# Weight-sum jobs summed one step behind their loads, with the full-size loads on GpSimd's queue

## The chip, the cores and the metric

The kernel runs on one core of a Trainium2 chip. The metric is the device time of one execution in microseconds; three runs of the kernel before took 1957.03, 1960.13 and 1961.34 us.

## The reference

One layer of a decoder for 1024 prompt tokens and 8 x 4 sample tokens, in float32. What matters here are its matrix products:

```python
h = rmsnorm(x, norm1_g) * (1.0 + sc1) + sh1
u = h @ w_in                      # u_x, u_g, u_q, u_k, u_v, u_r, u_lr, u_ga, u_gb
...                               # y_a: recurrent branch (conv, two gates per block, scan)
...                               # y_b: gated linear attention branch
m = sigmoid(u_ga) * (y_a @ proj_a) + sigmoid(u_gb) * (y_b @ proj_b)
x = x + gt1 * (m @ w_out)
h2 = rmsnorm(x, norm2_g) * (1.0 + sc2) + sh2
f1, f2 = split(h2 @ ffn_w1, 2)    # 22 tiles of 128 columns each
x = x + gt2 * ((silu(f1) * f2) @ ffn_w2)
```

## The kernel before

**Two halves.** The tokens are done in two halves: `A` (512 prompt tokens) and `B` (512 prompt tokens and the 32 sample tokens). Each half runs `begin` or the norm, `branches` (projections, attention, recurrent branch, `merge_b`, `merge_a`) and `back` (w_out, second norm, FFN). In the trace, tile names of half A end in a, those of half B in b.

**Three matmuls for one.** A float32 product is made of three matmuls: each weight tile is loaded into a buffer "raw" (512 KB as a rule), and split there into a high part (ScalarE, L154) and a low part (VectorE, L155), written to one of three "hl" buffers. `gemm` (L452 to L454) multiplies high by high, high by low and low by high. The raw buffer is free when the split is done, the hl buffer when the matmuls that read it are.

**Weight sums.** The products marked fast (`ffn1_fast`, `ffn2_fast`, `gates_fast`) multiply 2 x 2 blocks with seven products in place of eight. They need sums and differences of weight blocks. These are made once, while other stages run, and kept in DRAM (`wsum`, `wsumg`, `wsum2`). A *job* loads two weight tiles r1 and r2, does four additions on VectorE and stores both back:

- *Full-size jobs*, `weight_sums` (L348): for FFN tiles f = 6 to 21, two loads of 512 KB through SyncE's queue (`load_raw`, L145; the trace calls the tiles s_raw), sums in L352 to L355, two stores through GpSimd's queue (L356, L357). One `next(sums_of)` does all of it. They use the same five raw buffers as the weight loads.
- *Half-size jobs*, `paced_sums` (L362): twenty jobs for FFN tiles 4 and 5, the gate weights and part of the FFN's second weights, in two buffers of their own (tag "sums"). Loads go through GpSimd's queue (L388) behind a one-column copy (L387) from the tile that `pace` names, so that they do not start before that tile exists. One `next(sums_late)` does the loads, the next one the sums (L392 to L396) and stores (L398).

**Where the jobs are done.** `merge_b` (L1182) goes through j = 0 to 7: a gate product (gbps, the tile for j + 1 in half A), then the product with proj_b (pbps) and the join (L1211). In half A the remaining steps of the recurrent branch run between these: products ux and ug, and for every pair of blocks two small gate loads of 128 KB (lwa_raw, also in raw buffers; the matmuls of L1094 read the raw buffer itself). `merge_a` (L1273, half A) goes through j = 0 to 7: a gate product (gaps), two products with halves of proj_a (papsa with pa0 and pa1), the join and `keep_m`. Full-size jobs are done in half A alone: in `merge_b` at j = 0 to 6, in `merge_a` at j = 0, 1, 3, 4 and 6, and in the first FFN output product (`ffn2(0, 11)`, called in `back`, L1644) at j = 0, 2, 4 and 6. Half-size jobs are loaded and summed in `merge_b` (half A: j = 3 to 6; half B: every j) and `merge_a` (half A: j = 1 to 4) or `merge_a_fast` (half B).

**What sets the order.** Each engine has one list of instructions that it runs in order, and the framework writes the lists: at each point it takes, of the instructions that can run by its own estimates, the one that stands first in the program. A tile's buffer is given out when it is first written and is free after its last use. `behind(n)` holds an instruction on its engine behind the last one that the program wrote before it: in the half-size jobs it keeps the first addition from moving ahead. The first addition of a full-size job had no such hold. `as_written` fixes the order of the matmuls in the fast products, not in the two merges of half A.

Of the kernel before, what the change touches and what calls it, by code (L numbers as in the profile page):

```python
# [7 lines left out]
F32 = mybir.dt.float32  # L8
# [7 lines left out]
P = 128  # L16
# [38 lines left out]
def hybrid_layer(ctx, tc, I, O):  # L55
# [292 lines left out]
    def weight_sums():  # L348

        for f in range(FAST[0], NF):  # L350
            r1, r2 = load_raw(I["ffn1"][2 * f], 1024, f"s1{f}"), load_raw(I["ffn1"][2 * f + 1], 1024, f"s2{f}")
            dve.tensor_add(r2[:, 512:1024], r2[:, 0:512], r2[:, 512:1024])  # L352
            dve.tensor_sub(r2[:, 0:512], r1[:, 0:512], r2[:, 0:512])
            dve.tensor_sub(r1[:, 0:512], r2[:, 512:1024], r1[:, 0:512])
            dve.tensor_sub(r1[:, 512:1024], r1[:, 512:1024], r1[:, 0:512])  # L355
            pool.dma_start(wsum[f][:, 0:1024], r1)  # L356
            pool.dma_start(wsum[f][:, 1024:2048], r2)  # L357
            yield 1
# [3 lines left out]
    def paced_sums():  # L362
# [20 lines left out]
        for k, (u, src, to) in enumerate(jobs):  # L383
            r = [wp.tile([P, 768], F32, tag="sums", name=f"sums{k}{v}", bufs=2) for v in range(2)]
            rv = [t[:, :2 * u].rearrange("p (n u) -> p n u", n=2) for t in r]
            for v in range(2):
                pool.tensor_copy(r[v][:, 0:1], pace[0][:, 0:1])  # L387
                pool.dma_start(rv[v], src[v])  # L388
            yield 1
            r1, r2 = rv  # L390
            last = len(traced())
            dve.tensor_add(r2[:, 1], r2[:, 0], r2[:, 1])  # L392
            behind(last)
            dve.tensor_sub(r2[:, 0], r1[:, 0], r2[:, 0])
            dve.tensor_sub(r1[:, 0], r2[:, 1], r1[:, 0])
            dve.tensor_sub(r1[:, 1], r1[:, 1], r1[:, 0])  # L396
            for v in range(2):
                pool.dma_start(to[v], rv[v])  # L398
            yield 1

    sums_of, sums_late = weight_sums(), paced_sums()

    class Half:
# [778 lines left out]
        def merge_b(s):  # L1182
# [14 lines left out]
            for j in range(KD):  # L1197
# [3 lines left out]
                if s.hf or 3 <= j < 7:  # L1201
                    pace[0] = tgs[j]
                    next(sums_late, None)
# [9 lines left out]
                if s.hf or 3 <= j < 7:  # L1213
                    next(sums_late, None)
                if s.hf == 0 and j < 7:
                    next(sums_of, None)
# [56 lines left out]
        def merge_a(s):  # L1273
            s.m = []
            for j in range(KD):
                tg = s.gate_a(j)
                if 1 <= j < 5:
                    next(sums_late, None)
                s.join(j, tg, s.over(tg, s.branch_a(j)))
                s.keep_m(j)  # L1280
                if 1 <= j < 5:
                    next(sums_late, None)
                if j % 3 < 2 and j < 7:
                    next(sums_of, None)
# [537 lines left out]
```

## Time and profile before

| | |
|---|---|
| median of three runs | 1960.13 us (1957.03 to 1961.34) |
| profiled execution | 1958.39 us, its span 1956.6 us |
| mean granted TensorE clock | 0.997 |
| busy, share of the span | PE 98%, PEld 90%, DVE 70%, ACT 50%, POOL 7% |
| moved by DMA | 319 MB, mean 163 GB/s |
| `merge_b` of half A | about 259 to 453 us of the span |
| `merge_a` of half A | 452 to 559 us |
| `ffn2(0, 11)` of half A | 728 to 789 us |

A page of the profile and its views name a group of instructions by line, engine, operation and tiles, "out<-in". PE is the matmul queue of TensorE, PEld its weight loads, DVE VectorE, ACT ScalarE, POOL GpSimd, SP SyncE; a q behind the name means the engine's sequencer or its DMA queue. A list of waits has: who waited, for whom, microseconds in total, times, the longest. In a timeline, the square bracket is the idle time before an instruction and what ended it.

### The profile page before, as it was taken

The numbers are of one execution on the slowest core, as the hardware profiler recorded it, in microseconds if no ns is written. First come the engines' busy times: TensorE is split into PE (matmuls) and PEld (weight loads), VectorE is DVE, ScalarE is ACT, GpSimd is POOL, SyncE is SP. The second block draws the span as 40 slices with busy tenths as digits, with TensorE's granted clock in tenths as the row PEclk, the third lists the DMA queues.
The fourth block names the chain that finished last, engine by engine and source line by source line (L and its number), as shares of the span: only waits on it lengthen the run. The fifth ranks groups of instructions, "written<-read, shape, count | busy, mean of one in ns | idle before, by whom it ended". The sixth has DMA issues, their size and how long they took to land. (4 is left out here: it accounts for less than half of the span.)

```text
span 1956.6 us, 33960 instructions
## 1 busy us (share of the span) xinstructions
PE 1923.5 (98%) x13380; PEld 1754.8 (90%) x13380; DVE 1360.1 (70%) x2420; ACT 972.6 (50%) x1559; POOL 144.6 (7%) x279
## 2 busy tenths in 40 slices
PE   8999999998999999999999999999999999999997
PEld 5877777787899998998899998999999999999997
DVE  5648587765658774677664497786467688888867
ACT  4536376552235552555353366675245354656653
POOL 0000002111200000000000101031201000000000
PEclk9999999999999999999999999999999999999999
DMA  8344326567864467554331413334447534555553
GB/s 342 116 154 172 117 90 245 176 211 240 292 201 157 129 184 243 193 183 149 119 123 65 146 50 101 124 114 153 140 143 226 198 130 133 176 171 179 177 163 104
DMA packets 122240, 319.24 MB, mean 163 GB/s; under 512 B 14560, under 2 KB 29664, under 8 KB 122080
## 3 DMA queue, kind: packets, MB, share of 16 engines
q1 hardware_dynamic: 107536, 263.89, 41.6%
q0 software_dynamic: 14000, 52.62, 7.5%
q8 instruction: 105, 1.72, 0.4%
q10 hardware_dynamic: 544, 0.56, 0.1%
q14 instruction: 55, 0.45, 0.1%
HBM read 278.42 MB, written 38.59 MB: 162 GB/s over the span
## 5 line engine op out<-in xcount | busy, mean ns | idle before, releaser
L155 DVE TENSOR_TENSOR fwa_hl<-fwa,fwa_hl 128x1024 fp32r<-128x1024 f32 (+1 forms) x57 | 68.8, 1207 | 44.6 <-ACT fwa_hl L154 41.2
L155 DVE TENSOR_TENSOR fwb_hl<-fwb,fwb_hl 128x1024 fp32r<-128x1024 f32 (+1 forms) x64 | 77.2, 1207 | 27.7 <-ACT fwb_hl L154 27.4
L154 ACT ACTIVATE fwa_hl<-fwa 128x1024 fp32r<-128x1024 f32 (+1 forms) x57 | 59.3, 1040 | 44.0 <-PE fapsa L1436 10.8
L154 ACT ACTIVATE fwb_hl<-fwb 128x1024 fp32r<-128x1024 f32 (+1 forms) x64 | 66.6, 1041 | 23.4 <-PE fcpsb L1436 9.0
L452 PE MATMUL f3psa<-faa,f3a_hl 128*128 128x512 f32 x176 | 68.6, 390 | 0.6 <-ACT f3a_hl L154 0.6
L454 PE MATMUL f3psa<-faa,f3a_hl 128*128 128x512 f32 x176 | 68.5, 390 | 0.4 <-DVE f3a_hl L155 0.4
L453 PE MATMUL f3psa<-faa,f3a_hl 128*128 128x512 f32 x176 | 68.6, 390 | 0.0
L154 ACT ACTIVATE f3a_hl<-f3a_raw 128x768 fp32r<-128x768 f32 (+1 forms) x32 | 25.3, 792 | 55.7 <-PE f3psa L454 47.3
L155 DVE TENSOR_TENSOR f3a_hl<-f3a_raw,f3a_hl 128x768 fp32r<-128x768 f32 (+1 forms) x32 | 28.3, 888 | 17.0 <-ACT f3a_hl L154 16.7
L452 PEld LDWEIGHTS f3psa<-faa,f3a_hl 128*128 128x128 f32 x176 | 33.0, 188 | 7.8 <-ACT f3a_hl L154 1.0
L454 PEld LDWEIGHTS f3psa<-faa,f3a_hl 128*128 128x128 f32 x176 | 33.0, 188 | 7.6 <-DVE f3a_hl L155 0.9
L453 PEld LDWEIGHTS f3psa<-faa,f3a_hl 128*128 128x128 f32 x176 | 33.0, 188 | 6.8
L352 DVE TENSOR_TENSOR s_raw<-s_raw 128x512 f32<-128x512 f32 x16 | 11.1, 691 | 40.2 <-DMA s_raw<-in_ffn 40.2
L454 PE MATMUL wopsb<-mb,wob_hl 128*128 128x272 f32 x128 | 36.9, 288 | 0.0
L452 PE MATMUL wopsb<-mb,wob_hl 128*128 128x272 f32 x128 | 36.9, 289 | 0.0
L453 PE MATMUL wopsb<-mb,wob_hl 128*128 128x272 f32 x128 | 36.8, 288 | 0.0
L453 PE MATMUL wopsa<-ma,woa_hl 128*128 128x256 f32 x128 | 36.4, 284 | 0.0
L454 PE MATMUL wopsa<-ma,woa_hl 128*128 128x256 f32 x128 | 36.2, 283 | 0.0
L452 PE MATMUL wopsa<-ma,woa_hl 128*128 128x256 f32 x128 | 36.1, 283 | 0.0
L1621 POOL DMA_DIRECT2D out_yb<-yb x4 | 2.9, 720 | 407.5 <-DVE yb L1618 406.8
L452 PE MATMUL uxpsa<-h1a,uxpsa_hl 128*128 128x512 f32 x80 | 32.3, 403 | 0.0
L155 DVE TENSOR_TENSOR fvb_hl<-fvb,fvb_hl 128x768 fp32r<-128x768 f32 x28 | 26.8, 956 | 7.7 <-ACT fvb_hl L154 7.4
(2404 smaller groups left out, 7975.3 us busy)
## 6 DMA issues: line engine op xcount, KB each, us to landing
ada<-in_ada_w SPq DMA_DIRECT2D x48, 512.0 KB, 5.5
fwb<-wsum SPq DMA_DIRECT2D x72, 256.0 KB, 3.6
s_raw<-in_ffn SPq DMA_DIRECT2D x32, 512.0 KB, 4.1
wsum<-s_raw POOLq DMA_DIRECT2D x32, 512.0 KB, 3.9
fwa<-wsum SPq DMA_DIRECT2D x64, 256.0 KB, 3.3
fwb<-in_ffn SPq DMA_DIRECT2D x54, 256.0 KB, 3.6
fwa<-in_ffn SPq DMA_DIRECT2D x48, 256.0 KB, 3.2
woa_raw<-in_w_out SPq DMA_DIRECT2D x13, 512.0 KB, 3.5
```

Source lines behind the costliest of these rows:

```text
L154: act.activation(hl[:, 0, :n], raw[:, :n], AF.Copy)
L155: dve.tensor_sub(hl[:, 1, :n], raw[:, :n], hl[:, 0, :n].bitcast(F32))
L352: dve.tensor_add(r2[:, 512:1024], r2[:, 0:512], r2[:, 512:1024])
L452: pe.matmul(out, wh, x[:, o:o + w], start=st, stop=False)
L453: pe.matmul(out, wh, x[:, N + o:N + o + w], start=False, stop=False)
L454: pe.matmul(out, wl, x[:, o:o + w], start=False, stop=en)
L1621: (queues[j // 2 % len(queues)]).dma_start(out[:, j:j + 2, o:o + w], y2)
```

## The change

A class `Jobs` steps through a list of jobs: `step` does the sums and stores of the job begun in the step before, and then begins the next one (its loads); `finish` does the last sums. Full-size and half-size jobs both go through it, so each job is summed one step behind its loads.

- A full-size job loads r1 and r2 through GpSimd's queue in place of SyncE's, into the same five raw buffers, without a pacing copy. Its first addition is now held by `behind`.
- A half-size job keeps its two buffers, queue and pacing copy.
- `merge_b`, half A: full-size steps at j = 0 to 6 and a `finish` at j = 7; half-size steps at j = 3 to 7 (five begin, four are summed). Half B: one half-size step at each j, ahead of the product with proj_b.
- `merge_a`: half-size steps at j = 0, 1, 2 and a `finish` at j = 3; full-size steps at j = 0 to 4 and a `finish` at j = 5.
- `merge_a_fast`: one step after each of the four gate groups, and a `finish` after the loop; before, jobs also went on at j >= 4.
- `ffn2(0, 11)`: steps at j = 0, 2, 4, 6 and a `finish` behind the loop.

```diff
--- before.py
+++ after.py
@@ -345,17 +345,39 @@
 
         return t[:, :HP].rearrange("p (m u n) -> p m u n", u=2, n=P)[:, :, u, :]
 
-    def weight_sums():
-
-        for f in range(FAST[0], NF):
-            r1, r2 = load_raw(I["ffn1"][2 * f], 1024, f"s1{f}"), load_raw(I["ffn1"][2 * f + 1], 1024, f"s2{f}")
-            dve.tensor_add(r2[:, 512:1024], r2[:, 0:512], r2[:, 512:1024])
-            dve.tensor_sub(r2[:, 0:512], r1[:, 0:512], r2[:, 0:512])
-            dve.tensor_sub(r1[:, 0:512], r2[:, 512:1024], r1[:, 0:512])
-            dve.tensor_sub(r1[:, 512:1024], r1[:, 512:1024], r1[:, 0:512])
-            pool.dma_start(wsum[f][:, 0:1024], r1)
-            pool.dma_start(wsum[f][:, 1024:2048], r2)
-            yield 1
+    class Jobs:
+
+        def __init__(s, jobs):
+            s.jobs, s.sums = iter(jobs), None
+
+        def finish(s):
+            if s.sums:
+                s.sums()
+            s.sums = None
+
+        def step(s):
+            s.finish()
+            job = next(s.jobs, None)
+            if job:
+                s.sums = job()
+
+    def full_sums(f):
+        def begin():
+            r1, r2 = [wp.tile([P, 1024], F32, tag="raw", name=f"s{k}{f}_raw", bufs=5) for k in "12"]
+            for r, t in (r1, 2 * f), (r2, 2 * f + 1):
+                pool.dma_start(r, I["ffn1"][t])
+
+            def sums():
+                last = len(traced())
+                dve.tensor_add(r2[:, 512:1024], r2[:, 0:512], r2[:, 512:1024])
+                behind(last)
+                dve.tensor_sub(r2[:, 0:512], r1[:, 0:512], r2[:, 0:512])
+                dve.tensor_sub(r1[:, 0:512], r2[:, 512:1024], r1[:, 0:512])
+                dve.tensor_sub(r1[:, 512:1024], r1[:, 512:1024], r1[:, 0:512])
+                pool.dma_start(wsum[f][:, 0:1024], r1)
+                pool.dma_start(wsum[f][:, 1024:2048], r2)
+            return sums
+        return begin
 
     pace = [None]
 
@@ -380,25 +402,31 @@
         for c in range(GATES):
             columns(wsumg[c], [I["w_in"][T_GA + 2 * c + v] for v in range(2)])
         rows(1)
-        for k, (u, src, to) in enumerate(jobs):
+        return [half_sums(k, *job) for k, job in enumerate(jobs)]
+
+    def half_sums(k, u, src, to):
+        def begin():
             r = [wp.tile([P, 768], F32, tag="sums", name=f"sums{k}{v}", bufs=2) for v in range(2)]
             rv = [t[:, :2 * u].rearrange("p (n u) -> p n u", n=2) for t in r]
             for v in range(2):
-                pool.tensor_copy(r[v][:, 0:1], pace[0][:, 0:1])
+                if pace[0] is not None:
+                    pool.tensor_copy(r[v][:, 0:1], pace[0][:, 0:1])
                 pool.dma_start(rv[v], src[v])
-            yield 1
-            r1, r2 = rv
-            last = len(traced())
-            dve.tensor_add(r2[:, 1], r2[:, 0], r2[:, 1])
-            behind(last)
-            dve.tensor_sub(r2[:, 0], r1[:, 0], r2[:, 0])
-            dve.tensor_sub(r1[:, 0], r2[:, 1], r1[:, 0])
-            dve.tensor_sub(r1[:, 1], r1[:, 1], r1[:, 0])
-            for v in range(2):
-                pool.dma_start(to[v], rv[v])
-            yield 1
-
-    sums_of, sums_late = weight_sums(), paced_sums()
+
+            def sums():
+                r1, r2 = rv
+                last = len(traced())
+                dve.tensor_add(r2[:, 1], r2[:, 0], r2[:, 1])
+                behind(last)
+                dve.tensor_sub(r2[:, 0], r1[:, 0], r2[:, 0])
+                dve.tensor_sub(r1[:, 0], r2[:, 1], r1[:, 0])
+                dve.tensor_sub(r1[:, 1], r1[:, 1], r1[:, 0])
+                for v in range(2):
+                    pool.dma_start(to[v], rv[v])
+            return sums
+        return begin
+
+    sums_of, sums_late = Jobs([full_sums(f) for f in range(FAST[0], NF)]), Jobs(paced_sums())
 
     class Half:
         def __init__(s, hf):
@@ -1198,9 +1226,9 @@
                 n = f"{s.n}{j}"
                 if j + lag < KD:
                     first(j + lag)
-                if s.hf or 3 <= j < 7:
+                if s.hf or j >= 3:
                     pace[0] = tgs[j]
-                    next(sums_late, None)
+                    sums_late.step()
                 if j + lag < KD:
                     yield 5.2
                 tg = tgs.pop(j)
@@ -1210,10 +1238,8 @@
                 for (t, p), (o, _) in zip(s.over(tg, p2), s.over(m, p2)):
                     dve.scalar_tensor_tensor(o, t, 1.0, p, op0=OP.add, op1=OP.mult)
                 s.mb.append(m)
-                if s.hf or 3 <= j < 7:
-                    next(sums_late, None)
-                if s.hf == 0 and j < 7:
-                    next(sums_of, None)
+                if s.hf == 0:
+                    sums_of.step() if j < 7 else sums_of.finish()
                 yield 5.2
 
         def gate_a(s, j):
@@ -1274,14 +1300,12 @@
             s.m = []
             for j in range(KD):
                 tg = s.gate_a(j)
-                if 1 <= j < 5:
-                    next(sums_late, None)
+                if j < 4:
+                    sums_late.step() if j < 3 else sums_late.finish()
                 s.join(j, tg, s.over(tg, s.branch_a(j)))
                 s.keep_m(j)
-                if 1 <= j < 5:
-                    next(sums_late, None)
-                if j % 3 < 2 and j < 7:
-                    next(sums_of, None)
+                if j < 6:
+                    sums_of.step() if j < 5 else sums_of.finish()
 
         def merge_a_fast(s):
 
@@ -1304,7 +1328,7 @@
             product = s.products(units, 512, s.bs, "gw" + s.n)
             for c in range(GATES):
                 tgs = s.gates_fast(c, product)
-                next(sums_late, None)
+                sums_late.step()
                 if c == GATES - 1:
                     s.keep_m(*range(2 * c))
                 for i in range(2):
@@ -1312,9 +1336,7 @@
                     s.join(j, tg, [(tg[:, :N], held[j])] if j < 4 else s.over(tg, s.branch_a(j)))
                     if c == GATES - 1:
                         s.keep_m(j)
-                    if j >= 4:
-                        next(sums_late, None)
-            drain(sums_late)
+            sums_late.finish()
             as_written(begin, (mybir.EngineType.PE,))
 
         def residual(s, dst, ps, slot, j, src, part, name):
@@ -1643,7 +1665,8 @@
                 drain(s.ffn1_fast(range(FAST[0], 11)))
                 for j, _ in enumerate(s.ffn2(0, 11, s.whole)):
                     if j % 2 == 0:
-                        next(sums_of, None)
+                        sums_of.step()
+                sums_of.finish()
                 return
             s.fs = {k: [] for k in ("11", "21", "22", "t1", "t2", "t3", "t4")}
             mix(chain(s.ffn1_first(p1, EARLY), s.ffn2(0, 4, s.whole)), b)
@@ -1694,7 +1717,6 @@
     load_later()
     derive()
     A.branches(None)
-    drain(sums_of)
     A.act = {}
     drain(A.ffn1_fast(range(11, NF)))
     acc = [ACC("3a")]
```

## The prediction

> **What bounds the kernel now.** I read the page first. Its row of busy times:
>
> ```profile
> PE 1923.5 (98%) x13380; PEld 1754.8 (90%) x13380; DVE 1360.1 (70%) x2420; ACT 972.6 (50%) x1559; POOL 144.6 (7%) x279
> ```
>
> PE is busy 1923.5 of 1956.6 us. The change touches no matmul, so it can give back at most the idle 33 us and what a slower clock costs, but it can add any stall. So next I cut the span into stretches of 25 us and looked for those in which PE starts fewer matmuls (columns: stretch, length, then busy us and count of PE, PEld, DVE, ACT, POOL; clock, DMA share, GB/s):
>
> ```profile
> 450.00:475.00 25.00, 19.42 (x77) 15.31 (x76) 15.08 (x23) 4.39 (x6) 3.96 (x7) 0.90 0.62 220
> 475.00:500.00 25.00, 25.00 (x107) 20.52 (x107) 13.76 (x20) 6.69 (x9) 5.75 (x12) 0.96 0.75 246
> 500.00:525.00 25.00, 25.00 (x112) 20.70 (x111) 14.62 (x22) 7.32 (x10) 6.31 (x12) 1.00 0.91 333
> ```
>
> All three hold the same product, 128x512 matmuls of the first half's merges. 112 fit into 25 us undisturbed (0.223 us each); the first two hold 35 + 5 fewer. Those 40 matmuls, 8.9 us, are the one place where the full-size jobs cost time today. The timelines of PE and DVE show how:
>
> ```profile
> 465.85 0.39 PE L453 MATMUL gapsa<-h1a,gapsa_hl 128*128 128x512 f32 x1
> 471.10 0.79 PE L454 MATMUL gapsa<-h1a,gapsa_hl 128*128 128x512 f32 x1 [4.86 <-DVE gapsa_hl L155]
> ```
>
> ```profile
> 451.08 0.69 DVE L352 TENSOR_TENSOR s_raw<-s_raw 128x512 f32<-128x512 f32 x1 [5.50 <-DMA s_raw<-in_ffn]
> ...
> 467.77 0.69 DVE L352 TENSOR_TENSOR s_raw<-s_raw 128x512 f32<-128x512 f32 x1 [7.95 <-DMA s_raw<-in_ffn]
> ```
>
> ```profile
> 472.00:474.00 2.00, 2.00 (x6) 1.52 (x6) 2.00 (x4) 0.00 (x0) 0.49 (x1) 0.50 0.70 223
> 476.00:478.00 2.00, 2.00 (x8) 1.60 (x7) 0.00 (x0) 0.00 (x0) 0.00 (x0) 0.78 0.78 287
> ```
>
> DVE waits 7.95 us for a job's load, the split of the next gate weights (L155) stands behind it, PE starves 4.86 us, and afterwards it runs at clock 0.50 until about 476.5, some 5.5 us at half speed, 2.7 us lost. The list of waits has twelve such DVE waits; only the two around 451 and 468 reach PE:
>
> ```profile
> DVE s_raw L352 <- DMA s_raw<-in_ffn: 40.2, 12, 7.9
> ```
>
> The view that decides is the list of waits of SP's queue:
>
> ```profile
> SPq L145 <- DMA wsum<-s_raw: 86.5, 28, 9.6
> ...
> SPq L145 <- PE g2a L1094: 23.6, 7, 9.6
> ```
>
> The "raw" tag has five buffers for every weight load of SP and for the jobs' r1 and r2. 28 times a weight load could not start until a job's store had left its buffer, and seven times until the gate matmuls of the recurrent branch had left theirs. These waits end early enough today; buffers are nevertheless what SP's lead over PE is made of.
>
> **The change part by part.**
>
> *Sums one step later* removes the DVE wait in the merge: a load has a whole step to land (12.0 us, 54 matmuls of 0.223). Gain: the 8.9 us. The splits then stand behind nothing.
>
> *The pair is held longer.* Load and sums used to be in one step; now r1 and r2 stay occupied from the load to the end of the next step, sums and stores. How early is the load? Whether a load may go ahead of its place shows here, at a tag with 17 buffers:
>
> ```profile
> 892.96 1.09 POOL L541 DMA_DIRECT2D xb<-in_xb  x2 [119.71 <-ACT fwa_hl L154]
> ```
>
> ```profile
> L454 PE MATMUL f3psa<-faa,f3a_hl x88: 389/389/389, 729.0 to 788.2; 128*128 128x512 f32 x88
> ```
>
> The eleven activation tiles are read for the last time at 788, POOL sits idle 119.7 us, and still the xb loads start at 893: buffers had been kept for tiles that stand earlier in the program. So buffers are given out in program order. POOL's own instructions do pass each other, though: a copy of a later step (L387) runs ahead of a store of the earlier one (L356):
>
> ```profile
> 493.73 0.35 POOL L387 COPY sums<-gaa 128x1 f32<-128x1 f32 x1
> ...
> 495.83 0.55 POOL L356 DMA_DIRECT2D wsum<-s_raw  x1 [0.33 <-issue]
> ```
>
> I conclude that a job's two loads will take their buffers as soon as their turn comes, as today, and not wait for the stores of the job before. Four of five buffers are then held by two jobs, and one is left for all weights. Its turn-round is what I price.
>
> *Merge b, two places.* Behind two jobs stand the small gate loads of the recurrent branch, whose buffers are held until PE has used them:
>
> ```profile
> 296.99 7.38 SPq L145 DMA_DIRECT2D s_raw<-in_ffn  x2
> 304.46 1.26 SPq L145 DMA_DIRECT2D lwa_raw<-in_lru_w  x2
> ...
> 374.05 9.96 SPq L145 DMA_DIRECT2D s_raw<-in_ffn  x2
> 387.77 5.85 SPq L145 DMA_DIRECT2D lwa_raw<-in_lru_w  x2
> ```
>
> ```profile
> 325.74 1.02 PE L1094 MATMUL g1a<-xca,lwa_raw 128*128 128x512 f32 x2
> ...
> 329.84 0.50 PE L452 MATMUL gbpsa<-h1a,gbpsa_hl 128*128 128x512 f32 x1
> ```
>
> ```profile
> 325.94 0.69 DVE L1211 SCALAR_TENSOR_TENSOR mba<-gba,pbpsa 128x512 f32<-128x512 f32 x1 [0.51 <-PE pbpsa L454]
> ```
>
> ```profile
> DMA to landing us min/median/max: 2.0/2.5/4.3
> ```
>
> ```profile
> s_raw<-in_ffn SPq DMA_DIRECT2D x32, 512.0 KB, 4.1
> wsum<-s_raw POOLq DMA_DIRECT2D x32, 512.0 KB, 3.9
> ...
> sums<-in_ffn POOLq DMA_DIRECT2D x16, 384.0 KB, 4.9
> ...
> f3a_raw<-in_ffn SPq DMA_DIRECT2D x16, 384.0 KB, 3.6
> ...
> f3a_raw<-in_ffn SPq DMA_DIRECT2D x16, 320.0 KB, 3.1
> ...
> gbpsa_raw<-in_w_in SPq DMA_DIRECT2D x8, 512.0 KB, 3.7
> ...
> gapsa_raw<-in_w_in SPq DMA_DIRECT2D x8, 512.0 KB, 4.3
> ...
> pa0a_raw<-in_proj_a SPq DMA_DIRECT2D x8, 320.0 KB, 5.2
> pa1a_raw<-in_proj_a SPq DMA_DIRECT2D x8, 320.0 KB, 4.3
> ```
>
> ```profile
> L154 ACT ACTIVATE pba_hl<-pba_raw x8: 1047/1054/1063, 271.5 to 439.0; 128x1024 fp32r<-128x1024 f32 x8
> L155 DVE TENSOR_TENSOR pba_hl<-pba_raw,pba_hl x8: 1203/1218/1226, 272.9 to 443.0; 128x1024 fp32r<-128x1024 f32 x8
> ```
>
> The first fence is SP's timeline, then PE's and DVE's; the line on landing is that of the gate loads in this stage; the transfers have queue, count, KB and median us to landing; the last two rows are the split of a weight tile on ACT and DVE (ns min/median/max).
>
> With one buffer free the first gate load sits in it until its four matmuls end, 325.74 plus twice 0.86: 327.5. The older job's sums start behind the join at 325.94; with that join, one split (1.22) and two sums (0.69 each) its first store goes out near 329.3 and lands 3.9 later, at 333: too late. The second gate load goes at 327.5, lands 2.5 later at 330.0, and is used up at 331.7 (PE idle 2.5). Then gb: landing 3.7, ACT 1.05, DVE 1.22: ready by 337.0 to 337.7 where PE began it at 329.84. Loss 7.2, at both places: +14.4. The rest of merge b uses a weight each 5.4 us (24 matmuls) and gets one each 3.7 + 2.3 = 6.0: +2 for lags that add up (0 to 2). Bounds of the two places: 12 with landings of 2 and 3 us, 20 with 5; none of it if the gates stand elsewhere in PE's order.
>
> *Merge a.* A step has one gate and two proj_a loads, and now five jobs in a row (j = 0 to 4) instead of j = 0, 1, 3, 4, 6.
>
> ```profile
> L154 ACT ACTIVATE pa0a_hl<-pa0a_raw x8: 740/740/741, 447.2 to 543.9; 128x640 fp32r<-128x640 f32 x8
> L155 DVE TENSOR_TENSOR pa0a_hl<-pa0a_raw,pa0a_hl x8: 816/818/827, 455.8 to 544.6; 128x640 fp32r<-128x640 f32 x8
> ```
>
> One buffer's round: gate 4.3 + 1.05 + 1.22 = 6.6, proj_a 5.2 + 1.56 and 4.3 + 1.56; together 19.2 us, and 15.6 with landings near 3 (the f3a row has 3.1 for that size), against 12.0 of matmuls. The first two steps live on the weights that are split ahead; j = 3, 4, 5 pay. Nearest to the lower end, since a slower PE thins the traffic out: 4 each, +12 (3 to 22).
>
> *FFN second product.* A job every two tiles, four loads:
>
> ```profile
> 728.50:788.50 60.00, 60.00 (x267) 49.69 (x266) 30.24 (x41) 14.15 (x18) 3.74 (x7) 1.00 0.75 248
> ```
>
> 267 matmuls in 60 us, so 66 take 14.8. One buffer needs 2 x (3.6 + 1.8) + 2 x (3.1 + 1.56) = 20.1 (1.8 is an estimate between the two split sizes). Three such intervals, less two weights split ahead (18 matmuls, 4 us each): 3 x 5.3 - 8 = +8 (3 to 12).
>
> *Clock.* One stall in merge b is about as long as the 4.86 above, so its 2.7 us comes back: +2.7 (0 to 8). The Trainium skill (TensorE: Matmul & The Clock Gate, section What's actually happening) says that an idle window of about 3.4 us halves the clock until a busy window has passed; the trace agrees, 0.50 after 4.86 us. By it each long stall would cost about 1.7, an estimate from that page, and the sum would hardly move.
>
> *Loads through POOL* take 32 issues off SP, which spends them waiting, and cost POOL, 7% busy, 32 x 0.55 (the store row at 495.83) = 18 us beside everything else: 0. What is queued behind them on POOL are the copies of the convolution's history, for which DVE and in the end PE wait:
>
> ```profile
> POOL hist L1071 <- ACT uba L1064: 116.0, 8, 71.3
> ```
>
> POOL itself waits 116 us for ACT at these copies, and a load that waits there for a buffer delays them by at most one round of 6.6; PE reads the result two or three products later. 0, and 6 for the upper end, inside the 20 above. *Half-size jobs* have two buffers of their own and a copy that paces them; no PE wait stands on them today, so 0 in both halves. One of them (the last quarter of the gate sums) is now stored after the first round of the second half's fast gates; it is read in the fourth round, with two rounds of seven products between: 0. *Shifted columns* (j + 1 instead of j, and no gap at j = 2 and 5) leave the number of jobs as it was; what they cost is in the merge a term.
>
> Sum: -8.9 + 14.4 + 2 + 12 + 8 + 2.7 = +30. The profiled execution took 1958.4 (span 1956.6 and 1.8 around it), 1.7 under the median 1960.1 of the runs. 1958.4 + 30 = 1988.
>
> **The rivals.** *Faster:* the job's loads are put behind the stores of the job before on POOL's queue, as the code writes them. A pair is then taken late, weights keep three buffers, and only the gain is left: 1958.4 - 8.9 = 1949.5. For it: 28 waits on those stores cost PE nothing today. Against it: the two rows in which POOL's instructions pass each other. It decides if the pair's load starts later than the older pair's last store.
>
> *Same:* buffers do not bind, the DMA engines do. Four steps of merge a now move 4.8 MB in each 12.0 us (weights 1.2, full job 2.1, half job 1.6), 400 GB/s, where the stretch 500 to 525 moved 333 at a share of 0.91. At 333 a step takes 14.4: four times 2.4 gives back 9.6, time 1959. The Trainium skill (DMA: Bandwidth & Descriptors, section Issuing engines are not separate DMA queues) has loads from POOL and SP share the same 16 engines; it speaks for this case, and no run here shows it yet.
>
> *The change doesn't do what it says*, sums still waiting on DMA, has no row for it: a step is three times the landing of 4.1.
>
> **How the numbers follow.** Slower 0.68, at 1988 with its own range 1967 (lower ends 12 + 3 + 3 less 8.9) to 2013 (20 + 22 + 12 + 8 less 8.9, rounded up). Faster 0.24, at 1949.5. Same 0.08. The runs spread over 0.22%, so 0.2% is what can be told from no change. The range must reach to the faster case: 1949 to 2013.
>
> **What would show it.** Right: few DVE waits on s_raw; SP's waits on the stores of s_raw grow well over 86.5; PE waits on gbpsa_hl, gapsa_hl, papsa and f3a_hl between 325 and 560 and 735 and 800, with clock near 0.5 behind a gate pair. Wrong: PE starts 112 matmuls in each 25 us from 450 to 550, and PE's idle total falls below 33; then pairs are taken late, or PE's order hides the round.

## The result and the profile after

The change makes the kernel slower: 2027.39 us (2023.78 to 2028.52, five runs) against 1959.53 (1956.62 to 1961.34), a ratio of 1.0347 with a 95% interval of 1.0332 to 1.0362. The sign of the forecast was right, its size was less than half: 1988 was predicted, in a range that ended at 2013. The profiled execution has a span of 2026.0 us, 69.4 more than before. The row of busy times of the page after:

```profile
PE 1948.6 (96%) x13380; PEld 1765.8 (87%) x13380; DVE 1362.7 (67%) x2420; ACT 974.8 (48%) x1559; POOL 163.4 (8%) x311
```

The number of matmuls is the same, so the 69.4 us split into two parts at once. PE's busy time rose from 1923.5 to 1948.6, by 25.1 us for the same instructions. Its idle time rose from 33.1 to 77.4, by 44.3 us.

Next, the same view for stretches of the program. Both tables have, in this order, `merge_b`, `merge_a` and `ffn2(0, 11)` of the first half, the two FFN tiles behind it, and all the rest up to the end; the bounds are the starts of PE's first product in each. Columns: stretch, length, busy us and count of PE, PEld, DVE, ACT, POOL; clock, DMA share, GB/s. Before:

```profile
271.27:452.36 181.09, 181.09 (x793) 142.31 (x792) 133.57 (x195) 103.25 (x146) 32.90 (x56) 1.00 0.59 201
452.36:559.25 106.89, 101.31 (x434) 82.81 (x432) 61.39 (x89) 28.89 (x39) 18.64 (x36) 0.97 0.75 262
728.53:788.39 59.86, 59.86 (x266) 49.55 (x265) 30.21 (x41) 14.12 (x18) 3.74 (x7) 1.00 0.75 249
788.39:812.83 24.44, 24.44 (x206) 24.43 (x205) 16.14 (x22) 14.07 (x23) 0.00 (x0) 1.00 0.58 182
812.83:1956.62 1143.79, 1124.05 (x8794) 1093.96 (x8792) 827.06 (x1558) 589.20 (x998) 81.83 (x157) 1.00 0.45 143
```

After:

```profile
271.39:479.65 208.26, 189.28 (x793) 144.98 (x792) 134.33 (x192) 104.78 (x145) 41.03 (x66) 0.97 0.47 162
479.65:607.03 127.38, 107.43 (x434) 85.64 (x433) 63.09 (x92) 29.45 (x40) 24.98 (x48) 0.91 0.70 241
775.77:845.77 70.00, 62.53 (x267) 48.60 (x265) 28.28 (x40) 12.83 (x17) 6.42 (x12) 1.00 0.50 165
845.77:874.82 29.05, 27.88 (x205) 27.21 (x205) 20.05 (x27) 14.93 (x24) 1.06 (x2) 0.89 0.82 268
874.82:2026.00 1151.18, 1127.70 (x8794) 1096.41 (x8792) 826.59 (x1558) 589.70 (x998) 80.81 (x157) 0.99 0.45 142
```

Length less PE's busy time is idle time. The growth of the busy time is only in part the clock: `ffn2` has 2.7 us more of it at a granted clock of 1.00. What the clock takes can be estimated from slices of 1 us: busy time, times what the granted clock lacks of 1.00. That is 2.9 us before and 21.8 us after, so about 19 of the 25.1 (1.7 of it ahead of `merge_b`). The other 6 are, for the most part, waits too short to show as idle time, since in these rows a matmul counts as busy for 0.39 us while the next one starts some 0.23 us after it.

| stretch | longer by | idle | busy | of it the clock, an estimate |
|---|---|---|---|---|
| `merge_b`, first half | 27.2 | 19.0 | 8.2 | 5.9 |
| `merge_a`, first half | 20.5 | 14.4 | 6.1 | 4.9 |
| `ffn2(0, 11)` | 10.1 | 7.5 | 2.7 | 0.0 |
| two FFN tiles behind it | 4.6 | 1.2 | 3.4 | 3.0 |
| the rest to the end | 7.4 | 3.7 | 3.7 | 3.4 |

The three stages with full-size jobs and the two tiles behind them lost 62.4 of the 69.4 us; the two stretches not shown differ by under 0.6. The DMA engines are no busier: a share of 0.47 in `merge_b` where it was 0.59, 0.70 in `merge_a` after 0.75. PE's waits:

```profile
PE gapsa L480 <- ACT gapsa_hl L154: 14.6, 4, 9.7
PE gbpsa L480 <- ACT gbpsa_hl L154: 9.0, 2, 4.8
PE papsa L480 <- ACT pa0a_hl L154: 4.3, 1, 4.3
PE pbpsa L480 <- ACT pba_hl L154: 4.2, 1, 4.2
PE f3psa L480 <- ACT f3a_hl L154: 3.9, 4, 1.6
PE g1a L1122 <- DMA lwa_raw<-in_lru_w: 3.9, 2, 2.3
```

Each is a wait for a weight, and what ends it is the first split (ACT) or the landing itself, not the second split behind the sums on DVE: the weights come late. GpSimd's timeline of the full-size loads (L368) and stores (L377, L378) shows why:

```profile
404.57 0.56 POOL L368 DMA_DIRECT2D s_raw<-in_ffn  x1 [2.51 <-DVE uxpsa_hl L155]
406.31 0.54 POOL L368 DMA_DIRECT2D s_raw<-in_ffn  x1 [1.18 <-DVE ugpsa_hl L155]
...
433.58 0.53 POOL L368 DMA_DIRECT2D s_raw<-in_ffn  x1 [7.28 <-DVE gbpsa_hl L155]
438.31 0.55 POOL L368 DMA_DIRECT2D s_raw<-in_ffn  x1 [0.54 <-DVE ugpsa_hl L155]
...
459.50 0.56 POOL L378 DMA_DIRECT2D wsum<-s_raw  x1
...
460.75 0.58 POOL L377 DMA_DIRECT2D wsum<-s_raw  x1
```

The pair loaded at 404.6 is stored at 459.5; from 433.6 on the next pair is in the buffers too. This pair stays 55 us from load to store. The others stay 23 to 67 us, where before it was 8 to 21 for all jobs but the first. Four of the five raw buffers are taken for much of the two merges. The longest wait, 9.73 us before the gate product at 535.0, shows the whole chain: SyncE could start the load of these weights only at 527.75, after 12.3 us of waiting for the stores of an older pair, issued at 522.01 and 524.16.

### The profile page after: what moved, and what is told of

Same layout as the page of the kernel before. It is cut to its first block, busy times and chain, and to the rows that moved or that the text cites. A ratio compares the mean times of both kernels' runs of the same rounds, so it can differ in the third digit from the quotient of the medians.

```text
span 2026.0 us, 33973 instructions
## 1 busy us (share of the span) xinstructions
PE 1948.6 (96%) x13380; PEld 1765.8 (87%) x13380; DVE 1362.7 (67%) x2420; ACT 974.8 (48%) x1559; POOL 163.4 (8%) x311
## 5 line engine op out<-in xcount | busy, mean ns | idle before, releaser
L480 PE MATMUL gapsa<-h1a,gapsa_hl 128*128 128x512 f32 x64 | 28.0, 438 | 14.6 <-ACT gapsa_hl L154 14.6
L481 PEld LDWEIGHTS f3psa<-faa,f3a_hl 128*128 128x128 f32 x176 | 33.1, 188 | 6.6
L368 POOL DMA_DIRECT2D s_raw<-in_ffn x32 | 17.3, 539 | 249.9 <-DMA f3a_raw<-in_ffn 176.0
L480 PE MATMUL gbpsa<-h1a,gbpsa_hl 128*128 128x512 f32 x64 | 26.4, 412 | 9.0 <-ACT gbpsa_hl L154 9.0
```

The source lines that it names most:

```text
L368: pool.dma_start(r, I["ffn1"][t])
L480: pe.matmul(out, wh, x[:, o:o + w], start=st, stop=False)
L481: pe.matmul(out, wh, x[:, N + o:N + o + w], start=False, stop=False)
```

## The experiments

All ratios are to the kernel before, run beside them. Three readings were to be told apart. **Q**: the loads on GpSimd's queue do the harm. **B**: the pairs hold the raw buffers, and the weights wait. **P**: the half-size jobs, which the prediction priced at nothing, cost something of their own.

**1. Without the hold** (kernel after):

```diff
                 dve.tensor_add(r2[:, 512:1024], r2[:, 0:512], r2[:, 512:1024])
-                behind(last)
```

> Kernel after, without the hold on a full-size job's first addition; loads through GpSimd's queue and the step distance in the program stay. Theory B (buffers: a pair of raw buffers is held for about 45 us in the kernel after, about 14 us before, and the weights wait for them): the additions may again go soon after their loads, the pairs are held 13 to 25 us, and the time is 1950 to 1975 us. Rival Q (the loads on GpSimd's queue do the harm): over 2005 us, as they are still there.

Measured: 1977.49 us, ratio 1.0085 (1.007 to 1.01). Without the hold the first additions follow their loads by 4 to 8 us again, and a pair stays 10 to 22 us from load to store (all but the first). `merge_b` is 181.4 us long and `ffn2` 60.8, as before. 50 of the 68 us hang on the hold; the queue, unchanged here, has no part in those. The time is 2.5 us above B's range, and what makes up the 17.5 us that remain was not taken apart.

**2. Loads back on SyncE's queue** (kernel after):

```diff
-                pool.dma_start(r, I["ffn1"][t])
+                sp.dma_start(r, I["ffn1"][t])
```

> Kernel after, with the full-size loads back on SyncE's queue; additions stay one step behind and held. Theory B (buffers): the pairs are held as long as in the kernel after (30 to 65 us), 2010 to 2040 us. Rival Q (GpSimd's queue): under 1975 us.

Measured: 2030.76 us, 1.0355 (1.0337 to 1.0374). Q falls: with the queue undone the whole loss stays.

**3. GpSimd's queue alone** (kernel before):

```diff
-            r1, r2 = load_raw(I["ffn1"][2 * f], 1024, f"s1{f}"), load_raw(I["ffn1"][2 * f + 1], 1024, f"s2{f}")
+            r1, r2 = [wp.tile([P, 1024], F32, tag="raw", name=f"s{k}{f}_raw", bufs=5) for k in "12"]
+            for r, t in (r1, 2 * f), (r2, 2 * f + 1):
+                pool.dma_start(r, I["ffn1"][t])
```

> Kernel before, with nothing changed but that the full-size loads go through GpSimd's queue. Theory B (buffers): pairs held 13 to 20 us as before, 1953 to 1968 us. Rival Q (GpSimd's queue): over 1990 us.

Measured: 1966.94 us, 1.0042 (1.0026 to 1.0059). Inside B's range, and yet not nothing: `merge_a` is 5.0 us longer than before. The queue costs a little where VectorE still waits for the loads; why the loads come later there was not tried.

**4. The hold alone** (kernel before): `last = len(traced())` ahead of the first addition and `behind(last)` after it.

> Kernel before, with nothing changed but that the first addition of a full-size job is held behind the VectorE instruction written before it; loads and additions stay in one step, loads on SyncE's queue. Theory B (buffers): the pair is held up to its step's end instead of 14 us, 20 to 35 us; the VectorE waits for the loads (40.2 us) fall under 8; a part of the loss comes, 1965 to 2005 us. Rival Q (GpSimd's queue): under 1960 us, as the VectorE waits go and nothing else.

Measured: 1961.64 us, 1.0008 (0.9999 to 1.0017): no change that can be told. VectorE's waits for these loads are gone and the pairs, but for the first, are held 21 to 33 us from load to store. B in its simple form is wrong: a pair held twice as long costs nothing here, where 1965 to 2005 was expected. `merge_b` and `ffn2` of this kernel:

```profile
271.55:452.64 181.09, 181.09 (x794) 142.31 (x793) 133.29 (x193) 103.93 (x146) 30.69 (x54) 1.00 0.56 189
...
729.79:789.65 59.86, 59.86 (x266) 49.55 (x265) 32.26 (x44) 13.88 (x18) 4.26 (x8) 1.00 0.70 225
```

Here the next pair is loaded at most 14 us before the older one is stored, so that for the most part one pair is in the buffers. `merge_a`, however, does not win what the lost waits seemed to cost: it is 108.2 us long, 1.3 more than before, with 6.2 us of idle time. Its gate splits on VectorE now wait 17.2 us for ScalarE's splits, where it was 5.7: the weights come later. The next guess was that the second pair does the harm.

**5. The half-size part alone**: the kernel before with the class `Jobs`, `half_sums` and the new columns for the half-size jobs, and its own full-size jobs.

> Kernel before with the half-size jobs of the kernel after (one step behind, their new columns) and its own full-size jobs, on SyncE's queue. Theory P (the pacing copy reads the gate tile that the join writes in place, so the join on VectorE waits for the copy, which now waits for stores just issued): VectorE waits for POOL's copies 10 to 25 us (3.1 before), the first half's merge_a 4 to 9 us longer, the stretch behind the first half's FFN 4 to 8 us longer; 1966 to 1976 us. Rival (buffers of the full-size jobs are everything): 1957 to 1963 us.

Measured: 1976.62 us, 1.0079 (1.0053 to 1.0104). P holds in the main: the part priced at zero costs 0.8%, and the time is 0.6 us above its range. `merge_a` is 9.8 us longer, and there VectorE waits for the half-size loads, which P had not named; the rest behind `ffn2` is 9.9 longer, where joins wait for GpSimd's copies, as P had it. VectorE's longest waits in the stretch from 445 to 570, and in that from 1480 to 1560:

```profile
DVE sums L413 <- DMA sums<-in_ffn: 27.3, 4, 9.2
```

```profile
DVE gcb L1284 <- POOL sums L407: 12.0, 4, 5.2
```

**6. The full-size part alone**: the kernel after with the half-size jobs of the kernel before.

> Kernel after with the half-size jobs of the kernel before; full-size jobs as in the kernel after. Theory B and P together: merge_b and ffn2 of the first half as long as in the kernel after (+27 and +10), the last stretch back within 2 us of before; 2008 to 2020 us. Rival (the full-size jobs are everything): 2024 to 2031 us.

Measured: 2036.17 us, 1.0381 (1.0359 to 1.0402), above both ranges and more than the whole change. The last stretch is back within 0.2 us of before, as P had it, but `merge_b` is 37.8 us longer than before instead of 27.2. So the two parts do not add. In four steps of `merge_b` the old half-size sums stand ahead of the held full-size ones, and the pairs summed there are held 4 to 6 us longer; that this makes the difference was not tried.

**7. One pair at a time** (kernel after):

```diff
             for r, t in (r1, 2 * f), (r2, 2 * f + 1):
+                last = len(traced())
                 pool.dma_start(r, I["ffn1"][t])
+                behind(last)
```

> Kernel after, with each full-size load held on GpSimd's queue behind the last store written before it, so that two pairs never stand in the raw buffers at once (as in the faster rival of the prediction). Additions one step behind, held. Theory B (two pairs at once, four of five buffers, do the harm, not the length of the hold): merge_b and ffn2 within 3 us of before; what the half-size jobs cost remains; 1965 to 1982 us. Rival (the length of the hold does it): over 2000 us.

Measured: 2108.64 us, 1.0747 (1.0717 to 1.0776). It is the faster rival of the prediction, built, and it is the slowest kernel so far: the guess on two pairs falls, and so does the rival on the length of the hold, since the second to the fifth pair stay 34 to 44 us from load to store, against 51 to 63 in the kernel after. SyncE's waits, then `merge_b`, `merge_a` and `ffn2`:

```profile
SPq L145 <- DMA wsum<-s_raw: 225.1, 29, 19.2
```

```profile
271.17:516.99 245.82, 200.34 (x793) 150.50 (x792) 135.12 (x195) 102.62 (x144) 39.82 (x68) 0.89 0.40 142
516.99:670.65 153.66, 116.37 (x433) 88.71 (x433) 64.96 (x89) 29.95 (x41) 22.23 (x46) 0.86 0.55 193
840.13:928.93 88.80, 70.03 (x266) 54.27 (x265) 29.41 (x40) 13.77 (x18) 6.45 (x12) 0.90 0.40 137
```

The weight loads now wait 225 us for the stores. Three buffers are in no pair's hands meanwhile, and SyncE does not fill them: after 429 us, for example, it starts no load until 448.0, when the stores issued at 444.60 and 446.53 have gone out. The reading is that buffers are given out in program order, and the next pair, which is held back, stands ahead of the weights of the next step. This gives a third theory, **L**: what counts is how many buffers the weights can get *ahead of* the held additions, their lead. Three in experiment 4 (one pair of five), one in the kernel after (two pairs, as the next pair comes first in the program), none in this one.

**8. One pair, old half-size jobs**: as 7, with the half-size jobs of the kernel before.

> As the kernel before it in this list (one pair at a time, full-size jobs one step behind on GpSimd's queue), with the half-size jobs of the kernel before. Theories B and P: no wait of VectorE on a full-size load is left and no second pair, 1950 to 1964 us. Rival (GpSimd's queue or the length of the hold costs by itself): over 1970 us.

Measured: 2117.6 us, 1.08 (1.0774 to 1.0825), far above what B and P forecast. It is the loss of 7 again, and the old half-size jobs do not help.

**9 and 10. Two left, one left**: experiment 4 with four and with three raw buffers (`bufs` changes in the same way at the one other place that names it).

```diff
-        raw = wp.tile([P, 1024], F32, tag="raw", name=name + "_raw", bufs=5)
+        raw = wp.tile([P, 1024], F32, tag="raw", name=name + "_raw", bufs=4)
```

> Kernel before with the hold on the first addition (loads and additions in one step, loads on SyncE's queue) and four raw buffers in place of five. Theory L (buffers are given out in program order, so what counts is how many are left for the weights that stand ahead of the held additions: three with one pair of five, one with two pairs, none where the next pair waits for the stores): two left. First half: merge_b 3 to 18 us longer, ffn2 0 to 6 us longer, between the kernel with three left (0 and 0) and the kernel after (27 and 10). Rival (what hurts is two pairs in flight, or the step distance itself): under 3 us in both. The rest of the kernel also has one buffer less, so only these two stretches are read.

> The same with three raw buffers: one left. Theory L: merge_b 18 to 40 us longer and ffn2 6 to 16 us longer than before, as in the kernel after (27 and 10), though only one pair is held, loads and additions stand in one step and the loads are on SyncE's queue. Rival (two pairs in flight, or the step distance itself): under 10 us in merge_b.

One run each, 1997.91 and 2038.13 us. `merge_b` and `ffn2` with four buffers:

```profile
271.75:470.05 198.30, 188.00 (x793) 145.77 (x792) 136.52 (x198) 104.65 (x146) 34.59 (x55) 0.97 0.54 176
...
756.59:820.54 63.95, 61.04 (x266) 49.29 (x265) 30.16 (x42) 13.84 (x18) 3.43 (x7) 1.00 0.58 191
```

and with three:

```profile
272.87:488.99 216.12, 192.10 (x793) 145.57 (x792) 137.41 (x198) 105.39 (x145) 27.96 (x57) 0.95 0.48 165
...
787.11:861.78 74.67, 65.30 (x267) 49.36 (x265) 31.05 (x44) 12.84 (x17) 4.26 (x8) 0.98 0.56 185
```

| buffers left for the lead | kernel | `merge_b` longer by | `merge_a` longer by | `ffn2` longer by |
|---|---|---|---|---|
| three | 4 | 0.0 | 1.3 | 0.0 |
| two | 9 | 17.2 | 10.4 | 4.1 |
| one | 10 | 35.0 | 16.5 | 14.8 |
| one | after | 27.2 | 20.5 | 10.1 |
| none | 7 | 64.7 | 46.8 | 28.9 |

L orders the rows, `merge_a` too, for which nothing had been forecast. Experiment 10 loses about as much as the change does with one pair, one step and SyncE's queue. So the rivals (two pairs in flight, the step distance) are not needed for a loss of this size.

**13 and 14. The controls**: four and three buffers without the hold, the kernel before otherwise.

> Kernel before with four raw buffers and no other change (no hold): the control to the kernel with two buffers left. Theory L (the lead past a held pair counts): the pair lets go after 8 to 21 us, so the weights have four buffers most of the time: merge_b 0 to 8 us longer than before, ffn2 0 to 2, clearly under the 17.2 and 4.1 with the hold. Rival (a buffer fewer costs by itself, held or not): merge_b 12 to 22 us longer.

> Kernel before with three raw buffers and no other change (no hold): the control to the kernel with one left. Theory L: merge_b 5 to 24 us longer than before, ffn2 2 to 9, clearly under the 35.0 and 14.8 with the hold. Rival (fewer buffers cost by themselves, held or not): merge_b 28 to 42 us longer.

One run each, 1953.95 and 1972.84 us. `merge_b` and `ffn2` with four buffers, then with three:

```profile
270.99:452.08 181.09, 181.09 (x793) 142.41 (x792) 135.16 (x195) 104.01 (x146) 35.56 (x56) 1.00 0.58 199
...
724.42:784.29 59.87, 59.87 (x267) 49.58 (x266) 31.10 (x42) 14.36 (x18) 4.05 (x8) 1.00 0.74 247
```

```profile
272.55:457.36 184.81, 183.05 (x794) 142.07 (x792) 134.75 (x195) 103.56 (x144) 31.31 (x56) 1.00 0.57 195
...
735.88:800.76 64.88, 62.71 (x266) 50.28 (x265) 30.97 (x43) 13.85 (x18) 4.26 (x8) 0.97 0.66 218
```

Four buffers lose 0.0 us in `merge_b` without the hold and 17.2 with it, three lose 3.7 (a little under L's range) and 35.0. In `ffn2` it is 0.0 and 4.1, 5.0 and 14.8. Scarcity by itself explains only the smaller part: it is the hold, together with the buffers it leaves. This is what decides for L.

**11. Half-size steps behind the join** (experiment 5):

```diff
-                if j < 4:
-                    sums_late.step() if j < 3 else sums_late.finish()
                 s.join(j, tg, s.over(tg, s.branch_a(j)))
                 s.keep_m(j)
+                if j < 4:
+                    sums_late.step() if j < 3 else sums_late.finish()
...
                 tgs = s.gates_fast(c, product)
-                sums_late.step()
...
+                sums_late.step()
             sums_late.finish()
```

> The kernel with the half-size jobs alone (1976.6 us), with their steps moved in both merge_a: behind the join and the splits of m instead of between gate and join. Theory P (the step stands behind the gate's split, which runs ahead of its place, so VectorE comes to the additions too early, and the pacing copy holds the tile that the join has to write): VectorE's waits on half-size loads in the first half's merge_a fall from 27 us under 8, its waits on POOL's copies from 12 us under 3; 1957 to 1967 us. Rival (the new columns of the jobs cost): over 1970 us.

Measured: 1966.7 us, 1.0042 (1.0029 to 1.0056), at the upper end of P's range. About half of the cost (0.79%, now 0.42%) hung on the place of the step: `merge_a` is 1.5 us longer than before, not 9.8, and no wait for GpSimd's copies shows among VectorE's longer waits. Those for the half-size loads in `merge_a` fall only from 27.3 to 14.0, not under 8.

**15. The same edit in the kernel after.**

> Kernel after with the half-size steps of both merge_a behind the join and the splits of m. If the half-size jobs' waits add to those of the buffers: VectorE's wait of 9.5 us in merge_a and the waits for GpSimd's copies go, merge_a 5 to 9 us shorter than in the kernel after, the rest 3 to 5 us shorter, 2013 to 2021 us. If the two hide each other (the weights are late anyway): 2022 to 2035 us.

Measured: 2037.93 us, 1.0395 (1.0377 to 1.0413). VectorE's waits for GpSimd's copies and the 9.5 us in `merge_a` are gone, and `merge_a` is 136.6 us long, not shorter than 127.4. The time lies above both ranges, 10.5 us over that of the change. So in the change itself, taking these waits away wins nothing. That they hide behind weights that are late anyway fits this; why the kernel became slower is open. The stretch behind `ffn2` is 6.8 us longer than before where it was 7.4: P's second half, the copies there, is not confirmed either.

**12. One full-size job moved** (kernel before):

```diff
-                if j % 3 < 2 and j < 7:
+                if j in (0, 3, 4, 6):
...
-                    if j % 2 == 0:
+                    if j in (0, 2, 4, 5, 6):
```

> Kernel before with one full-size job moved out of merge_a (j = 0, 3, 4, 6 instead of 0, 1, 3, 4, 6) into ffn2 (j = 0, 2, 4, 5, 6). The job of j = 1 is the one whose load wait of 7.95 us reached PE. If its going takes that stall away and ffn2 hides one more job: 1950 to 1957 us. If the stall passes to the next job: 1957 to 1963.

Measured: 1957.02 us, 0.9986 (0.9976 to 0.9996), faster than both kernels. `merge_a` and `ffn2`:

```profile
452.33:550.57 98.24, 98.22 (x434) 81.02 (x432) 57.70 (x83) 28.86 (x39) 16.91 (x33) 1.00 0.75 264
719.54:780.91 61.37, 60.52 (x267) 49.40 (x265) 32.38 (x45) 14.05 (x18) 4.79 (x9) 1.00 0.78 262
```

`merge_a` has lost 8.65 us and all of its idle time; `ffn2` gave back 1.5. Of this the median shows 2.7: the stretch behind the FFN, which the job does not touch, happens to have 3.2 us more busy time in this profile than in that of the kernel before. The stall that the change was to remove needed one job less at that place, not a longer way for all jobs.

**16 and 17. Four buffers, timed**: experiment 13 again, and experiment 12 with four buffers.

> Kernel before with four raw buffers, as in the control, now timed in rounds. The one run gave 1953.95 us, with merge_a 3.4 us shorter. If that holds: 1953 to 1958 us. If it was the scatter of one run: 1958 to 1963.

> Kernel before with the job moved out of merge_a (1957.0 us) and four raw buffers. Theory L: without a hold a fifth buffer is not needed in merge_b; merge_a stays without idle time, ffn2 with five jobs loses 1 to 5 us: 1953 to 1960 us. If the fifth buffer is what hides the fifth job in ffn2: 1960 to 1970.

Measured: 1956.79 us, 0.9987 (0.9975 to 0.9998), and 1958.22, 0.9996 (0.9984 to 1.0007). The fifth buffer buys nothing in the kernel before; the two gains do not add. Experiments 12 and 16 cannot be told apart.

## Why the prediction was wrong in size

The forecast's terms can be set against the table of stretches. Taking the clock's 2.7 out of its gain of 8.9, the prediction had 30.2 us of waits for weights (6.2 less, 14.4 + 2, 12, 8) and nothing net for the clock. Measured were 50.5 (44.3 of idle time and 6.2 that PE counts as busy) and about 19. The mechanism was right. Of the 39 us that were missing, 20 lie in the waits, in `merge_a` above all, and 14 in the clock of the stages concerned. The other 5 are clock in stretches (1.7 ahead of `merge_b`, 3.4 in the rest to the end) where kernel 4, which leaves both alone, also has 2.4 and 3.2 us more busy time than the kernel before: mostly scatter.

- **The clock term failed: +2.7 predicted, 16.7 us lost in these stages.** The failed step is "One stall in merge b is about as long as the 4.86 above, so its 2.7 us comes back". It charged one stall, though the prediction's own terms have five of 4 us and more (two places in merge b, three steps in merge a). In the kernel after, the clock fell at eight stalls between 271 and 875 us. The gate products at 535.0, 551.1 and 567.8, for example, took 7.49, 7.94 and 8.12 us from first to last matmul where 5.60 is undisturbed, and waits inside them make up none, 0.53 and 0.53 us of that. The rows under "What the hardware showed" are of the second.
- **Merge a was sized too low: idle 20.0 us against 5.6 before, so +14.4, where 12 less 6.2 makes +5.8.** The round of one buffer was priced right (15.6 to 19.2 us; the gates that start at 535.0, 551.1 and 567.8 are 16.1 and 16.7 apart). So was what "j = 3, 4, 5 pay": these rounds were 3.9, 4.5 and 2.5 us longer than 12.2, 10.9 in all with the clock, where 12 was forecast. The failed step is "The first two steps live on the weights that are split ahead", which put the rounds before at nothing: j = 0, 1 and 2 were 1.2, 7.5 and 9.9 us longer. That lead was not there: at 471.3, 8 us before merge a began, PE had already waited 4.2 us for a weight. Moving the half-size sums (experiment 15) did not shorten it.
- **Merge b's two places held.** At each, PE idled 6.4 to 6.5 us (1.65 + 4.75 and 2.27 + 4.20) where 7.2 was forecast (331.7 + 3.7 + 1.05 is 336.5, so the terms up to the first split make 6.6). The +2 for the rest of merge b was low: 19.0 less 12.9 leaves 6.1, 4.2 of it before a product with proj_b (the pbpsa row). The mechanism, one buffer left for all weights, is what experiments 4, 7, 9, 10, 13 and 14 show.
- **The second FFN product held:** +8 forecast, 10.1 us there, 7.5 of it idle time, and none the clock. Of the idle time 3.1 us stand at its end, before the first product of the next tile; there the clock fell and cost 3.0 us behind it, for which the sum had no term.
- **Half-size jobs were priced at zero, "no PE wait stands on them today".** Experiment 5 puts them at 13.6 us by themselves. Within the change, neither the old half-size jobs (6) nor moved ones (15) made the kernel faster, so no run shows that the zero made the sum wrong. Two things were not read in the diff. The hold ties the sums to the VectorE instruction written before; in `merge_a` this had been the split of m at the end of a step and now is the split of the gate's weights, which runs a step ahead of its place. So VectorE reaches the sums too early and waits, with the next weight splits behind it. In the kernel after:

```profile
495.25 0.56 DVE L419 TENSOR_TENSOR sums<-sums 128x384 f32<-128x384 f32 x1 [9.52 <-DMA sums<-in_ffn]
...
497.50 1.22 DVE L155 TENSOR_TENSOR gapsa_hl<-gapsa_raw,gapsa_hl 128x1024 fp32r<-128x1024 f32 x1
```

  PE's wait behind it ends with ScalarE's split, so it is the weight that came late there:

```profile
498.13 0.80 PE L480 MATMUL papsa<-yaa,pa0a_hl 128*128 128x512 f32 x1 [4.31 <-ACT pa0a_hl L154]
```

  And the pacing copy reads a column of the gate tile that the join then overwrites, so the join waits for a copy that itself waits for the stores just issued (VectorE's waits in the kernel after; before, 2.9 and 0.2):

```profile
DVE gcb L1290 <- POOL sums L413: 11.4, 4, 5.3
...
DVE gaa L1290 <- POOL sums L413: 7.0, 3, 4.6
```

- **Loads through GpSimd: 0** is right within the change (experiment 2); by itself the queue costs 7 us (experiment 3).
- **The gain of 8.9 us did not come.** Its size is right for the stall: with the job gone (experiment 12), `merge_a` is 8.65 us shorter. The step to it failed, "The splits then stand behind nothing": experiment 4 removes VectorE's waits and keeps the job, and `merge_a` is 1.3 us longer, since the splits then stand behind weights that come later.
- **The faster rival (0.24) rested on a wrong step,** "A pair is then taken late, weights keep three buffers". Held back behind the stores, a pair keeps the weights back with it (experiment 7). The row of 892.96 that the prediction quotes for its own case already said so: buffers are given out in program order.
- **Of the signs that it named,** PE's waits on gbpsa_hl, gapsa_hl, pa0a_hl and f3a_hl came, as did the end of VectorE's waits on s_raw. SyncE's waits on the job's stores, which were to grow well over 86.5 us, fell:

```profile
SPq L145 <- DMA wsum<-s_raw: 56.2, 16, 12.3
...
SPq L145 <- PE g2a L1122: 51.7, 8, 13.9
```

  With one buffer left, a weight waits for the weight before it: the waits for the gate matmuls, which read a raw buffer themselves, went from 23.6 to 51.7. A list of waits names the last to let go of a buffer, not the one that keeps the others.

Not settled: why the old half-size jobs beside the new full-size ones are slower still (6), and what the 3.7 us of idle time in the rest to the end come from, since they outlast the waits for the copies. The 3.7 us of busy time there are mostly scatter: kernel 12, which leaves that stretch alone, has 3.2 more than the kernel before, as kernel 4 has.

## What to carry to other kernels

Where loads for side work share buffers with a stream that must run ahead, count how many buffers the stream can get *ahead of* the point at which the side work lets go, in the order in which buffers are given out; here, in one stage, three cost nothing, two cost 17 us and one cost 27 to 35. Prefer to thin the side work out at the one place where it hurts (one job moved: ratio 0.9986, 0.9976 to 0.9996) over lengthening the way of every job. And where a forecast has several long stalls, charge the clock for each of them and not once: here eight of the nine stalls of 1.8 us and more between 271 and 875 us brought it down, and none of the seven of 0.7 to 1.65.

## What the hardware showed

The granted clock fell without a long gap. PE's rows around 551 in the kernel after, and the slices of 1 us (columns as above):

```profile
551.10 0.50 PE L480 MATMUL gapsa<-h1a,gapsa_hl 128*128 128x512 f32 x1 [1.83 <-ACT gapsa_hl L154]
...
552.36 0.80 PE L482 MATMUL gapsa<-h1a,gapsa_hl 128*128 128x512 f32 x1 [0.53 <-DVE gapsa_hl L155]
```

```profile
551.00:552.00 1.00, 0.73 (x2) 0.30 (x2) 0.92 (x1) 0.57 (x2) 0.00 (x0) 0.98 0.01 4
552.00:553.00 1.00, 0.64 (x2) 0.54 (x3) 1.00 (x3) 0.00 (x0) 0.00 (x0) 0.50 0.00 0
...
555.00:556.00 1.00, 1.00 (x5) 0.79 (x4) 0.69 (x1) 0.64 (x1) 0.08 (x2) 0.82 0.43 152
```

After 1.83 us of idle time and two matmuls the clock fell to 0.50, about 0.1 us into the next idle time (the 0.98 of the slice that ends at 552), and stayed there for some 3.4 us. The product took 1.8 us more than undisturbed, its inner wait left out. The Trainium skill (TensorE: Matmul & The Clock Gate, section What's actually happening) halves the clock after an idle window of about 3.4 us; here the slow time is about as long as such a window, but 1.83 us of idle time in a row were enough.

Not every stall had this price. Between 271 and 875 us of the kernel after, PE stood still sixteen times for 0.7 us or more. The clock fell at eight of these, of 1.83 to 9.73 us. It stayed at 1.00 at one of 2.27 us and at the seven of 1.65 us or less, those inside `ffn2` among them. What decides between 1.83 and 2.27 us is not shown. In all the clock took about 19 us more than before, beside 44.3 us of idle time.
